# One block of A turned by DMA instead of TensorE, and the order of the first products that wait for it

## The chip, the cores and the metric

The kernel runs on one core of one Trainium2 chip. The metric is the device time of one execution in microseconds (us). A profile of one execution comes with the times. Its engines are called PE (TensorE), DVE (VectorE), ACT (ScalarE), POOL (GpSimd) and SP (the engine that only issues transfers here).

## The reference

```
x = a @ b                                  # 2048 x 2048 x 2048, float32 in
rms = sqrt(mean(x**2, axis=-1) + eps)      # one number for each row
out = gamma * x / rms                      # float32 out
```

## The kernel before, in words

**The product.** A is cut into 16 blocks of 128 rows, B into two halves of 1024 columns. TensorE needs A with the summed dimension on the partitions, so each block of A is turned (transposed) before it is used. Blocks 0 to 3 (the "head") are turned on TensorE while B still arrives. From block 4 on, two blocks make a group `g`, and each pair of a group and a half of B is computed by the Winograd form of Strassen's method: seven products of half size instead of eight, each 8 matmuls of 128x512, accumulated in banks of PSUM. `halves` numbers the pairs: n = 0 and 1 are the two halves of group 2 (blocks 4 and 5), n = 2 and 3 those of group 3 (blocks 6 and 7), and so on. `do(n, m)` issues product m of pair n. Products 1, 2 read quarters of the even block, so they need block 4 alone for n = 0 and 1; products 7, 6, 5, 3 read sums that `a_sums` makes on DVE from both blocks of the group, and product 4 a quarter of the odd block.

**Copies between products.** Several products go on accumulating on a copy of an earlier one. After product 1 ACT copies its bank to a second bank (`b2<-b1`, L591), after product 6 it copies that bank to a third (`b3<-b2`, L593), and products 5 and 3 go on in the third. `take(n, 11)` (L601) then copies the first bank to the result tile in SBUF. The banks are reused: pair n = 2 begins (product 1) in the bank that `take(0, 11)` has emptied into tile x_103, and x_103 must first have been stored to HBM with the previous rows that it held.

**How block 4 to 15 get turned.** A block is loaded as float32 (`load_block`, one transfer of 1 MB, issued by POOL), ACT takes the norms of its rows (`row_norm`), and DVE scales it to 16 bits. Blocks 4 and 5 are then turned on TensorE (`transpose_half`, L198, 8 transposes of 128x128 for each half) and copied from PSUM by `take_transposed` (L205). Blocks 6 and later go through `prepare` (L248 to L253): DVE scales each half (L252) and SP issues a transfer that turns it (`dma_start_transpose`, L253), two for each block.

**Rows finished.** `finish(mb)` multiplies a finished block by gamma and by its inverse norm on DVE (L314) and stores each half from SP (L317, 512 KB).

**What sets the order.** The schedule is by hand: each engine runs its instructions in the order of the program text. So a transfer of SP waits for all that stands before it on SP. On POOL, `wait_for` (L146) is a small copy that waits for a piece of data, and with it holds back the loads that stand behind it. Around the change the loads of blocks 6, 7 and 8 are issued one after the other (blocks 7 and 8 by the lines 550 and 620), and TensorE runs, after the last products of the head: block 4's transposes, four matmuls of `product_4`, do(0,1), block 5's transposes (`turn_next`), two more of `product_4`, do(0,2), do(0,7), do(0,6), do(1,1), do(0,5), do(0,4). Then `segment(1)` begins: do(1,6), do(0,3), do(1,2), do(2,1), do(1,7), do(1,5), do(1,4), and `segment(2)` with do(2,6).

Both kernels hold the same loop of the later groups; the short names below are used in what follows: T4 to T7 for the turning of blocks 4 to 7, load 6 to load 8 for the loads of these blocks.

Of the kernel before, what the change touches and what calls it, by code (L numbers as in the profile page):

```python
# [17 lines left out]
def kernel(  # L18
# [13 lines left out]
    nc = tc.nc  # L32
# [61 lines left out]
    def at(mb):  # L94
        return (at_even, at_odd)[(mb // 2) % 2][:, mb % 2]

    def copy_on(engine):
        return nc.scalar.copy if engine == "A" else nc.vector.tensor_copy

    def add(out, in0, in1, op=ALU.add):  # L100
        nc.vector.tensor_tensor(out=out, in0=in0, in1=in1, op=op)  # L101
# [30 lines left out]
    def load_block(mb):  # L132
        if mb == HB + 4:
            a32[mb] = head_flat[:, 2 * K:].bitcast(FP32)
        else:
            a32[mb] = a_pool.tile([P, K], FP32, name="a32")
        nc.gpsimd.dma_start(out=a32[mb], in_=a[mb * P:(mb + 1) * P, :])
# [7 lines left out]
    def wait_for(src):  # L145
        nc.gpsimd.tensor_copy(out=pace, in_=src)  # L146
# [47 lines left out]
    def transpose_half(mb, h, bank):  # L194
        view = bank.bitcast(FP16).rearrange("p (g m) -> p g m", m=P)
        for n in range(8):
            kt = h * 8 + n
            nc.tensor.matmul(  # L198
                view[:, n, :], a16[mb][:, kt * P:(kt + 1) * P], identity_h,
                is_transpose=True, start=(n == 0), stop=(n == 7),  # L200
            )
        return view

    def take_transposed(mb, h, view, copy):
        copy(out=at(mb)[:, h * 8:(h + 1) * 8, :], in_=view)  # L205
# [38 lines left out]
    def row_apply(mb):  # L244
        a16[mb] = a16_slot[mb]
        nc.vector.tensor_scalar_mul(out=a16[mb], in0=a32.pop(mb), scalar1=factor.pop(mb))
# [31 lines left out]
    def square_half(mb, h):  # L278
        square_of(mb, x_tile(mb, h))
# [4 lines left out]
    def take_pre(mb):  # L284

        pre_of[mb] = stat_pool.tile([P, 1], FP32, name="pre")
        add(pre_of[mb], msq[mb][:, 0:1], msq[mb][:, 1:2])
# [11 lines left out]
    def square_right(mb):  # L299

        square_half(mb, 1)
        rms_of[mb] = root(msq[mb][:, 2:3], pre_of.pop(mb))
# [6 lines left out]
    def finish(mb, order=(0, 1)):  # L309
        if mb not in inverse_of:  # L310
            inverse_of[mb] = inverse(rms_of.pop(mb))
        for h in order:
            x = x_half.pop((mb, h))
            nc.vector.scalar_tensor_tensor(  # L314
                out=x, in0=x, scalar=inverse_of[mb], in1=gamma_sb[:, h * HALF:(h + 1) * HALF],
                op0=ALU.mult, op1=ALU.mult)
            nc.sync.dma_start(out=rows(mb, h * HALF, (h + 1) * HALF), in_=x)  # L317
# [128 lines left out]
    def evict(groups, engines):  # L446
        for g, engine in zip(groups, engines):
            copy_on(engine)(out=x_chunk(*g), in_=banks[g])  # L448
# [85 lines left out]
    row_apply(HB)  # L534
    evict(plain[1:2], "D")
    row_factor(HB + 1)
    evict(plain[2:3], "A")
    product(PAIR, 1, 3, acc[0])
    product(PAIR, 1, 5, u4, start=False)

    def product_4(lo, hi):
        for kp in range(lo, hi):
            product_matmul(PAIR, 1, 4, u2, kp, False)
# [2 lines left out]
    turned = [transpose_half(HB, h, (tbank, acc[1])[h]) for h in range(2)]  # L546
    take_transposed(HB, 0, turned[0], nc.scalar.copy)
    take_transposed(HB, 1, turned[1], nc.vector.tensor_copy)
    row_apply(HB + 1)
    load_block(HB + 3)  # L550
    for r in range(HB):
        take_pre(r)
    evict(plain[3:], "A")
    square_right(0)
    product_4(2, 6)

    def turn_next():
        for h in range(2):
            view = transpose_half(HB + 1, h, (tbank, acc[2])[h])
            take_transposed(HB + 1, h, view, nc.vector.tensor_copy)  # L560

    def pair_ends():
        nc.scalar.copy(out=x21, in_=p7)
        nc.scalar.copy(out=x12, in_=u4)
        add(x22, x12, x21)
        add(x12, acc[0], x12)
        add(x21, u2, x21)

    halves = [(g, j) for g in range(G0, NG) for j in range(2)]
    B1, B2, B3, B7 = (acc[1], acc[0]), acc[3:5], (acc[6], acc[5]), acc[2]

    def chunks(n):
        g, j = halves[n]
# [2 lines left out]
    def do(n, m, copies=True):  # L578

        if n >= len(halves) or n < 0:  # L580
            return
        g, j = halves[n]
        b1, b2, b3 = B1[n % 2], B2[n % 2], B3[n % 2]
        if g >= G2:
            b1 = b2
        product(g, j, m, {1: b1, 2: b1, 3: b3, 4: b2, 5: b3, 6: b2, 7: B7}[m],
                start=m in (1, 7))
        if m == 1 and g >= G2:
            nc.scalar.copy(out=chunks(n)[0], in_=b2)
        elif m == 1:  # L590
            nc.scalar.copy(out=b2, in_=b1)  # L591
        elif m == 6:
            nc.scalar.copy(out=b3, in_=b2)  # L593
        elif m == 7 and copies:
            nc.scalar.copy(out=chunks(n)[2], in_=B7)  # L595

    def take(n, what, engine="A"):

        x11, x12, x21, x22 = chunks(n)
        if what == 11:  # L600
            copy_on(engine)(out=x11, in_=B1[n % 2])  # L601
        elif what == 12:
            copy_on(engine)(out=x12, in_=B3[n % 2])
        elif what == 22:
            add(x22, B3[n % 2], x21)
        else:
            add(x21, B2[n % 2], x21)
# [5 lines left out]
    def first_segment():  # L613
        n, g, j = 0, G0, 0
        nxt = 2 * g + 2
        do(n, 1)
        square_right(1)
        turn_next()
        product_4(6, KP)
        load_block(HB + 4)  # L620
        a_sums(g, (3, 1, 2), False)
        do(n, 2)
        do(n, 7, False)
        pair_ends()
        finish(0, (1,))
        row_norm(nxt)
        a_sums(g, (4,))
        prepare(nxt)
        finish(0, (0,))
        do(n, 6)  # L630
        do(n + 1, 1)
        do(n, 5)
        nc.scalar.copy(out=chunks(n)[2], in_=B7)
        take(n, 22)
        row_norm(nxt + 1)
        take(n, 11)
        finish(1)
        do(n, 4)
        take(n, 21)
        prepare(nxt + 1)  # L640
        square_half(2 * g + 1, j)

    X2, W2, Y2 = tbank, B1[1], B1[0]
# [5 lines left out]
    def segment(n):  # L649
        g, j = halves[n]  # L650
        ra, rb, nxt = 2 * g, 2 * g + 1, 2 * g + 2
        more = g + 1 < NG
        if g >= G2 and (g - G2) % 2 == 1 and j == 0:
            block_segment(n)
            return
        first = g >= G2 and (g - G2) % 2 == 0
        do(n, 6)
        own = nxt + (g == NG - 2)
        if j == 0:
            finish(ra - 1)  # L660
            row_norm(own)
        elif g == G0:
            square_right(r2)
        do(n - 1, 3)
        take(n - 1, 12)
        if j == 0:
            square_right(ra - 2)
            prepare(own)
            a_sums(g, (4,))
            finish(ra - 2, (0, 1) if g < NG - 2 else (0,))  # L670
        else:
            if not first:
                square_half(ra, 0)
            if g == G0:
                square_right(r3)
                finish(r2, (1, 0))
            elif g == G0 + 1:
                finish(r3, (1,))
            elif g == G2:
                b_two(4)  # L680
            elif not first and g > G2:
                finish(ra - 2)
        if g < G2:
            do(n, 2)
            take(n, 11)
        if g == G2 - 1 and j == 1:
            b_two(3)
            b_two(1)
        do(n + 1, 1)
        if j == 1 and g + 2 < NG:  # L690
            wait_for(at(nxt + 1)[:, KT - 1, 0:1])
            if G0 < g < NG - 3:
                load_block(nxt + 2)
                wait_for(a32[nxt + 2][:, 0:1])
            load_block(nxt + 3)
        if j == 1:
            if first:
                a_two_sums(g)
            a_sums(g + 1, (1, 2))
        do(n, 7)  # L700
        if j == 0 and g < NG - 2:
            row_norm(nxt + 1)
        if j == 1:
            a_sums(g + 1, (3,))
            if g == NG - 3:
                row_norm(nxt + 2)
        do(n, 5)
        take(n, 22)
        if j == 0 and g == NG - 2:
            finish(ra - 2, (1,))  # L710
        if j == 1:
            take_pre(rb)
            if not first:
                take_pre(ra)
        do(n, 4)
        take(n, 21)
        if j == 0:
            square_half(rb, 0)
            if g < NG - 2:
                prepare(nxt + 1)  # L720
            if g == G2:
                b_two(2)
        else:
            if g == NG - 3:
                prepare(nxt + 2)
            if not first:
                square_right(rb)
            if g == G0:
                finish(r3, (0,))
# [189 lines left out]
```

## Time and profile before

| | |
|---|---|
| median of 3 runs | 219.24 us (219.06 to 219.25) |
| the profiled execution | 219.5 us, of which the span is 217.7 |
| PE busy | 207.3 us, 95% of the span |
| DVE busy | 161.2 us, 74% |
| ACT busy | 112.9 us, 52% |
| POOL busy | 36.5 us, 17% |
| mean granted clock of PE | 0.992 |
| HBM read, written | 34.60 MB, 16.78 MB |

All times inside the profile count from the start of the span. A busy PE is one whose matmuls follow each other; the matmul records overlap, since one of 128x512 has a record of 379 ns and the next begins about 216 ns after it. The two lines of a group that tell most are its busy time and what ended the idle time before it.

### The profile page before, as it was taken

How to read it: one execution, taken by the hardware profiler on the slowest of the kernel's cores; microseconds unless marked ns; L12 is line 12 of the kernel's file. 1: busy time of each engine (PE TensorE's matmuls, PEld its weight loads, DVE VectorE, ACT ScalarE, POOL GpSimd, SP SyncE). 2: the span in 40 equal slices, each digit the busy share in tenths (PEclk: the TensorE clock that was granted, in tenths of full speed). 3: DMA queues.
4: the chain of work that ended last, by engine and by line, in shares of the span. 5: the costliest groups of instructions: out<-in, count | busy, mean ns of one | idle time of the engine just before them, and what ended most of it. 6: DMA issues, size and time to landing. Idle time of an engine off the chain costs nothing.

```text
span 217.7 us, 2953 instructions
## 1 busy us (share of the span) xinstructions
PE 207.3 (95%) x1000; PEld 96.9 (45%) x1020; DVE 161.2 (74%) x323; ACT 112.9 (52%) x222; POOL 36.5 (17%) x74
## 2 busy tenths in 40 slices
PE   7999999999999999999999999999999999999970
PEld 3545444444455444444444444444444444444420
DVE  1228669999887996989975899399859973385771
ACT  2110001810399566789635962585778551555771
POOL 7544333443001000200021001102020000000020
PEclk9999999999999999999999999999999999999996
DMA  7999999999948889889775985498995950040455
GB/s 149 168 200 207 199 205 205 209 208 212 397 201 266 327 218 308 243 350 246 228 220 173 359 252 96 193 225 263 293 301 157 288 217 0 0 193 3 193 189 196
DMA packets 37039, 46.60 MB, mean 214 GB/s; under 512 B 22560, under 2 KB 26656, under 8 KB 35744
## 3 DMA queue, kind: packets, MB, share of 16 engines
q0 software_dynamic: 10608, 23.86, 45.3%
q1 hardware_dynamic: 26144, 22.29, 34.5%
q10 hardware_dynamic: 272, 0.26, 0.3%
q8 instruction: 8, 0.13, 0.2%
q14 instruction: 7, 0.06, 0.1%
HBM read 34.60 MB, written 16.78 MB: 236 GB/s over the span
## 4 chain that ended last, share of the span: by engine, by line
PE 84%; DMA 9%; POOL 2%; issue 1%; ACT 1%; DVE 0%; ACTq 0%; POOLq 0%
PE acc L361 65%; PE acc L409 11%; DMA early<-in_a_dram 5%; DMA b<-in_b_dram 4%; PE acc L400 3%; PE tbank L400 2%; POOL b L115 1%; PE tbank L361 1%; PE tbank L438 1%; PE tbank L185 1%; POOL early L119 1%; ACT a L786 1%; PE acc L198 0%; PE tbank L198 0%; ACT sq L872 0%
## 5 line engine op out<-in xcount | busy, mean ns | idle before, releaser
L361 PEld LDWEIGHTS <-s 128*128 128x128 f16 (+1 forms) x312 | 30.5, 98 | 36.8
L275 ACT ACTIVATE sq<-x 128x1024 bf16<-128x1024 f32 (+1 forms) x33 | 33.2, 1006 | 19.6 <-DVE x L101 15.8
L409 PE MATMUL acc<-b,head_at 128*128 128x512 bf16 x171 | 42.1, 379 | 0.2
L314 DVE SCALAR_TENSOR_TENSOR x<-x,r,gamma_sb 128x1024 f32<-128x1024 f32 x28 | 35.0, 1281 | 0.5
L361 PE MATMUL acc<-b,head_at 128*128 128x512 bf16 x135 | 33.9, 379 | 0.3
L101 DVE TENSOR_TENSOR x<-acc,x 128x512 f32<-128x512 f32 x33 | 22.1, 686 | 11.4 <-PE acc L361 5.5
L361 PEld LDWEIGHTS <-head_at 128*128 128x128 f16 (+1 forms) x192 | 18.7, 98 | 22.2
L361 PE MATMUL acc<-b,at_even 128*128 128x512 bf16 x110 | 26.2, 379 | 0.1
L409 PEld LDWEIGHTS <-head_at 128*128 128x128 bf16 x176 | 16.9, 98 | 19.3 <-issue 0.3
L361 PE MATMUL acc<-early,s 128*128 128x512 bf16 x101 | 25.1, 379 | 0.1
L361 PEld LDWEIGHTS <-at_even 128*128 128x128 f16 x160 | 15.6, 98 | 19.0 <-ACT at_even L205 0.3
L361 PE MATMUL acc<-b,s 128*128 128x512 bf16 x99 | 23.8, 379 | 0.2
L227 ACT ACTIVATE sq<-a 128x1024 bf16<-128x1024 f32 x22 | 23.3, 1057 | 1.3 <-DMA a<-in_a_dram 0.9
L361 PE MATMUL acc<-t_left,s 128*128 128x512 bf16 x96 | 22.5, 379 | 0.1
L115 POOL DMA_DIRECT2D b<-in_b_dram x32 | 17.2, 540 | 20.0 <-DMA b<-in_b_dram 13.6
L448 ACT COPY x<-acc 128x512 f32<-128x512 f32 x7 | 4.0, 586 | 27.0 <-PE acc L409 27.0
L593 ACT COPY acc<-acc 128x512 f32<-128x512 f32 x12 | 6.9, 576 | 10.3 <-PE acc L361 10.3
L190 DVE COPY head_at<-tbank 128x1024 bf16<-128x1024 bf16 x7 | 4.8, 692 | 7.9 <-PE tbank L185 7.9
L296 DVE RECIPROCAL r<-rms 128x1 f32<-128x1 f32 x16 | 2.5, 159 | 10.6 <-ACT rms L291 10.6
L789 POOL TENSOR_SCALAR x<-x,r 128x512 f32<-128x512 f32 x2 | 1.4, 688 | 47.8 <-DVE r L296 47.8
L101 DVE TENSOR_TENSOR x<-tbank,x 128x512 f32<-128x512 f32 x9 | 6.2, 690 | 4.2 <-PE tbank L438 4.1
L595 ACT COPY x<-acc 128x512 f32<-128x512 f32 x10 | 5.8, 585 | 4.9 <-PE acc L361 3.8
(129 smaller groups left out, 243.7 us busy)
## 6 DMA issues: line engine op xcount, KB each, us to landing
out_dram<-x SPq DMA_DIRECT2D x29, 512.0 KB, 3.3
a<-in_a_dram POOLq DMA_DIRECT2D x9, 1024.0 KB, 5.6
b<-in_b_dram POOLq DMA_DIRECT2D x32, 256.0 KB, 10.0
a<-in_a_dram POOLq DMA_DIRECT2D x4, 512.0 KB, 9.8
early<-in_a_dram POOLq DMA_DIRECT2D x7, 256.0 KB, 10.0
gamma_sb<-in_gamma_dram POOLq DMA_DIRECT2D x2, 512.0 KB, 9.9
head_at<-in_a_dram POOLq DMA_DIRECT2D x1, 1024.0 KB, 7.1
out_dram<-x SPq DMA_DIRECT2D x3, 256.0 KB, 2.6
```

Source lines behind the costliest of these rows:

```text
L101: nc.vector.tensor_tensor(out=out, in0=in0, in1=in1, op=op)
L115: nc.gpsimd.dma_start(out=raw[j][kp][:, t, :], in_=b[lo:lo + P, j * HALF:(j + 1) * HALF])
L190: nc.vector.tensor_copy(out=head_at[:, 2 * kp:2 * kp + 2, :, :], in_=view)
L227: nc.scalar.activation(out=junk, in_=a32[mb][:, h * HALF:(h + 1) * HALF], func=ACTF.Square, scale=2.0 ** -8, accum_out=n2[:, h:h + 1])
L275: nc.scalar.activation(out=sq[:, 0:src.shape[-1]], in_=src, func=ACTF.Square, scale=inv_sqrt_n, accum_out=msq[mb][:, c:c + 1])
L314: nc.vector.scalar_tensor_tensor(out=x, in0=x, scalar=inverse_of[mb], in1=gamma_sb[:, h * HALF:(h + 1) * HALF], op0=ALU.mult, op1=ALU.mult)
L361: nc.tensor.matmul(bank, lhsT[:, kp, :], rhs, start=(start and kp == 0), stop=(kp == KP - 1), skip_group_check=not start)
L400: nc.tensor.matmul(bank, lhsT[:, k, :], rhs, start=(m in (1, 7) and k == 0), stop=(k == KQ - 1), skip_group_check=m not in (1, 7))
L409: nc.tensor.matmul(bank, head_at[:, kt, r, :], head_rhs(c, kt), start=(kt == 0), stop=(kt == KT - 1))
L448: copy_on(engine)(out=x_chunk(*g), in_=banks[g])
L593: nc.scalar.copy(out=b3, in_=b2)
L595: nc.scalar.copy(out=chunks(n)[2], in_=B7)
```

## The change

Block 5 is no longer turned on TensorE. DVE scales its two halves one by one and SP issues a transposing transfer for each (new L551 and L552), as for the blocks behind it. A `wait_for` on the turned block now stands on POOL ahead of load 7, and load 8 follows load 7 at once. On TensorE, `product_4` is no longer split around the transposes, and do(1,1) and do(1,2) move up, so that the order is do(0,1), do(1,1), do(0,2), do(1,2), do(0,7), do(0,6), do(0,5), do(0,4). do(1,1) goes to the bank `tbank` that the transposes used. ACT's eviction of one bank of the head goes to DVE, the adds of `pair_ends` and the store of block 0's right half move ahead of `a_sums`, the fourth sum and one half of `finish(1)` move back, and `take(1, 11)` moves behind do(2,1).

```diff
     evict(plain[1:2], "D")
     row_factor(HB + 1)
-    evict(plain[2:3], "A")
     product(PAIR, 1, 3, acc[0])
     product(PAIR, 1, 5, u4, start=False)
...
-    row_apply(HB + 1)
+    src, f = a32.pop(HB + 1), factor.pop(HB + 1)
+    for h in range(2):
+        half = slice(h * HALF, (h + 1) * HALF)
+        nc.vector.tensor_scalar_mul(out=a16_first[:, half], in0=src[:, half], scalar1=f)
+        nc.sync.dma_start_transpose(at(HB + 1)[:, h * KP:(h + 1) * KP, :], a16_first[:, half])
+    wait_for(at(HB + 1)[:, KT - 1, 0:1])
     load_block(HB + 3)
     for r in range(HB):
         take_pre(r)
+    product_4(2, KP)
+    load_block(HB + 4)
+    nc.scalar.copy(out=x21, in_=p7)
+    nc.scalar.copy(out=x12, in_=u4)
     evict(plain[3:], "A")
-    square_right(0)
-    product_4(2, 6)
-
-    def turn_next():
-        for h in range(2):
-            view = transpose_half(HB + 1, h, (tbank, acc[2])[h])
-            take_transposed(HB + 1, h, view, nc.vector.tensor_copy)
-
-    def pair_ends():
-        nc.scalar.copy(out=x21, in_=p7)
-        nc.scalar.copy(out=x12, in_=u4)
-        add(x22, x12, x21)
-        add(x12, acc[0], x12)
-        add(x21, u2, x21)
+    add(x22, x12, x21)
+    add(x12, acc[0], x12)
+    add(x21, u2, x21)
+    evict(plain[2:3], "D")
...
+    def b1_of(n):
+        return tbank if n == 1 else B1[n % 2]
...
         do(n, 1)
+        square_right(0)
+        do(n + 1, 1)
         square_right(1)
-        turn_next()
-        product_4(6, KP)
-        load_block(HB + 4)
+        do(n, 2)
+        do(n + 1, 2)
+        finish(0, (1,))
         a_sums(g, (3, 1, 2), False)
-        do(n, 2)
         do(n, 7, False)
-        pair_ends()
-        finish(0, (1,))
         row_norm(nxt)
-        a_sums(g, (4,))
         prepare(nxt)
         finish(0, (0,))
         do(n, 6)
-        do(n + 1, 1)
         do(n, 5)
         nc.scalar.copy(out=chunks(n)[2], in_=B7)
         take(n, 22)
+        a_sums(g, (4,))
         row_norm(nxt + 1)
         take(n, 11)
-        finish(1)
+        finish(1, (0,))
         do(n, 4)
         take(n, 21)
         prepare(nxt + 1)
+        finish(1, (1,))
         square_half(2 * g + 1, j)
...
-        if g < G2:
+        if g < G2 and n > 1:
             do(n, 2)
             take(n, 11)
...
         do(n + 1, 1)
+        if n == 1:
+            take(n, 11)
```

More of the change, by code (lines that the diff above doesn't have):

```diff
@@ L582, in do @@
         g, j = halves[n]
-        b1, b2, b3 = B1[n % 2], B2[n % 2], B3[n % 2]
+        b1, b2, b3 = b1_of(n), B2[n % 2], B3[n % 2]
         if g >= G2:
@@ L600, in take @@
         if what == 11:
-            copy_on(engine)(out=x11, in_=B1[n % 2])
+            copy_on(engine)(out=x11, in_=b1_of(n))
         elif what == 12:
```

## The prediction

> **What bounds the kernel now.** I read the chain that ended last first, then the same chain in order of time, then each engine's timeline around the change, then the transfers. The chain by engine and by line (shares of the span):
>
> ```profile
> PE 84%; DMA 9%; POOL 2%; issue 1%; ACT 1%; DVE 0%; ACTq 0%; POOLq 0%
> PE acc L361 65%; PE acc L409 11%; DMA early<-in_a_dram 5%; DMA b<-in_b_dram 4%; PE acc L400 3%; PE tbank L400 2%; POOL b L115 1%; PE tbank L361 1%; PE tbank L438 1%; PE tbank L185 1%; POOL early L119 1%; ACT a L786 1%; PE acc L198 0%; PE tbank L198 0%; ACT sq L872 0%
> ```
>
> TensorE is the bound, and in order of time (start, length) the chain has no wait around the change:
>
> ```profile
> 67.80 0.45 PE tbank L198 x8
> 68.25 0.45 PE acc L198 x8
> 68.74 10.96 PE acc L361 x50
> ```
>
> So whatever leaves TensorE's queue is gained, and any wait on it is lost. The two L198 rows are block 5's transposes. The rows that a new wait would come from are ACT's copies and the matmuls after which they stand:
>
> ```profile
> 74.34 0.57 ACT L593 COPY acc<-acc 128x512 f32<-128x512 f32 x1 [1.03 <-PE acc L361]
> 83.31 0.59 ACT L601 COPY x<-acc 128x512 f32<-128x512 f32 x1 [1.92 <-DVE s L237]
> 84.50 1.89 PE L361 MATMUL acc<-b,head_at 128*128 128x512 bf16 x8
> ```
>
> L593 is the copy after do(0,6), L601 is take(0,11), the last row is do(2,1), which needs L601's bank. L601's idle time is put down to a DVE step that was long done; what it waited for is the store of x_103, issued at 79.94 and landing 3.3 us later, at 83.27. Last, the loads of blocks 6, 7 and 8 on POOL:
>
> ```profile
> 64.36 0.53 POOL L137 DMA_DIRECT2D a<-in_a_dram  x1 [9.20 <-ACT norm L230]
> 67.97 0.53 POOL L137 DMA_DIRECT2D a<-in_a_dram  x1 [3.08 <-ACT rms L291]
> 69.42 0.53 POOL L137 DMA_DIRECT2D head_at<-in_a_dram  x1 [0.92 <-PE acc L361]
> ```
>
> They land 5.2, 5.5 and 7.1 us after issue, at 69.6, 73.5 and 76.5: before T6 is issued (77.16).
>
> **Removed from TensorE.** The two L198 rows: 0.45 + 0.45 = 0.90 us, all on the path. With them go two DVE copies (L205, 0.69 each), while DVE gets an eviction (0.69) from ACT; both have room there, so nothing.
>
> **New wait 1: a copy that loses its cover.** do(0,5) accumulates on the bank that L593 fills from do(0,6)'s result. Before, do(1,1) stood between do(0,6) and do(0,5): 1.73 us of matmuls (8 of 0.216) hid the copy. Now do(1,1) is ahead and do(0,5) follows do(0,6) directly. In the rows, do(0,6)'s eight slots end at 74.14, the copy runs from 74.34 to 74.91; so the next product waits 0.77, and some 0.1 for the hand-over (block 4's copies L205 ended at 65.73 and 65.86 and do(0,1) began at 65.91). Taken: 0.85 us; bounds 0.75 and 0.95. It eats the gain: -0.90 + 0.85 = -0.05.
>
> **New wait 2: is block 5 turned in time?** T5's first half is scaled when DVE has finished L205 (65.86): L252's 0.744 gives 66.53, the second half 0.77 later. SP issues T5a at 66.60; T6's two issues stand 1.45 apart (77.16, 78.61), so T5b at 68.05. T6b to T9b, undisturbed, land 4.5 to 4.85 after their block's first issue: 71.1 to 71.45. But load 6 is in flight until 69.56. The trace has two pairs issued into a load. At 144.02 the load landed at 146.93, the pair at 149.72, 2.8 later. The other:
>
> ```profile
> 151.85 1.24 SPq L253 DMA_TRANSPOSE at_even<-a_half  x1
> 153.26 3.18 SPq L253 DMA_TRANSPOSE at_even<-a  x1
> ```
>
> landed at 158.46, 1.8 after its load (156.65). The DMA queue table of the window 152.9 to 155.0 has one line (packets, MB, share of 16 engines), POOL's queue alone:
>
> ```profile
> q0 software_dynamic: 77, 0.63, 85.8%
> ```
>
> So a transfer that is issued behind a load is served after it. For T5b that gives 71.4 to 72.4; I take 71.8, with 71.1 to 72.4 as ends. On TensorE, 38 matmuls (six of `product_4`, four products) now stand from 64.97 on: 38 x 0.216 = 8.2, so do(0,7) is due at 73.17 and do(0,6) at 74.90. `a_sums` makes its three sums at 0.72 apart from 71.9: 72.6, 73.3, 74.0. In time by 0.5 and 0.9. Cost 0; each us by which T5b is later than 72.4 costs one.
>
> At this step stands a rule that speaks against the change. The row: 16 transposes in 0.90 us, 0.056 each. The Trainium skill, "VectorE: DVE Perf Modes", section "Rules for kernel authors", says to turn 128x128 on TensorE where PSUM will do as the destination and by DMA otherwise, and "The three transpose paths" gives 390 ns against 1309 ns. An estimate from that page would be 6.2 us off TensorE and 21 us until block 5 is there, some 14 us too late; the trace's pair needs 4.5 to 4.85, so I don't use it.
>
> **New wait 3: the loads move into T6.** Loads 7 and 8 now stand behind `wait_for` on T5b. T7 landed at 88.8 in the trace, its L146 began at 88.89 and the load behind it was issued at 89.53: 0.73 after landing. So load 7 goes out at 72.55 (4.6 later than before) and load 8 directly behind (0.53 of issue). Load 8 landed 8.55 after load 7's issue (67.97 to 76.5): now 81.1. Meanwhile T6 is ready at about its old time. On ACT, `row_norm(6)` now stands behind the copy after do(1,1) (69.9) and `square_right(1)`, so it begins near 71.9 and, with 2.66 as in the trace, ends at 74.6; DVE needs 0.7 from L235 to L252 and 0.74 for that: T6a at 76.1, T6b at 77.5. Both go behind load 8. By the two pairs above they land 1.8 to 2.8 after it: 82.9 to 83.9. Behind T6 on SP and in its queue is x_103's store. In the trace it landed 1.27 after T6b (82.0 to 83.27): now 84.2 to 85.2, mid 84.7, where 83.27 stood before. L601's copy and hand-over (0.04 + 0.58 + 0.1) let do(2,1) begin at 85.4. TensorE is due there at 84.50 - 0.90 + 0.85 = 84.45 (before, it had 0.6 to spare). Stall 0.95; with both T5 ends 71.1 to 72.4 and 1.8 to 2.8 it is 0 to 2.05.
>
> A rule weighs on this. The row: two stores issued at 119.58 and 120.78, into a load, land after 4.3 us where others take 2.6 to 3.3, and of 120.4 to 121.2 the queue table shows POOL's queue alone:
>
> ```profile
> q0 software_dynamic: 38, 0.31, 106.4%
> ```
>
> The skill's "DMA: Bandwidth & Descriptors", section "Rules for kernel authors", says that rings of two engines interleave by packet on the same 16 engines. By that, T6's packets of 256 bytes would pass one by one between load 8's of 8 KB, and nearly all of T6 would still come after it: the same sum, within 0.1. The trace shows no interleaving.
>
> **What follows.** ACT's chain after L601 (squares, L291, then DVE's L314 and `a_sums` of group 3, done at 90.92, 7.61 after L601's start) feeds do(2,6), which began at 91.41, 6.91 after do(2,1). With L601 at 84.75 the sums come at 92.36, and do(2,6) at 85.4 + 6.91 = 92.31 waits another 0.1. Later loads are paced by their own blocks and move along; T7 queues behind the two stores and lands near 89.3, ahead of its use at 91.5.
>
> **Sum.** -0.90 + 0.85 + 0 + 0.95 + 0.1 = +1.0. The profiled execution, 219.5 (span 217.7 and 1.8 around it), is 0.26 above the median; on the median 219.24 + 1.0 = 220.2.
>
> **Rivals.** *Not slower:* the DMA engines serve T6 and x_103's store ahead of load 8, or load 8 is quick. It decides at a landing of x_103's store by 83.75: then do(2,1) starts at 84.45, and the sum is -0.90 + 0.85 = -0.05, 219.2. For it: T5b at its early end with the short gap reaches 83.5. Against: no transfer in this trace passes a load. Chance 0.22. *T5 late:* a pair blocked on SP for 2.4 to 3.2 us, as in the two rows; T5b at 73.6 leaves the first sum at 74.4 against 73.17 (1.2 lost), and x_103's store at 86.5, do(2,1) at 87.2: +2.75 in all, 222.0. For it: load 6 is in flight; against: it ends soon after T5a. Chance 0.13. *Faster:* wait 1 is smaller than read and wait 3 absent. Even a free hand-over leaves L593's 0.57, so -0.3; more than the 0.44 (0.2%, about what a measurement of this kernel can tell from no change) needs a slack that I don't see. Chance 0.05. The forecast has 0.60.
>
> **The numbers.** Forecast, with T5b's and the gap's ends: 219.2 to 221.3. To reach 8 in 10 the range takes in the on-time case and most of the late one: 219.0 to 221.9. Faster by over 0.2%: 0.06. Within: 0.24 (on time 0.20 and the low end of the forecast 0.04). Slower: 0.70.
>
> **What would show it.** In the profile after: no L198 on block 5; a TensorE gap of 0.85 before do(0,5), ended by the copy after do(0,6); load 7 issued near 72.6; T6 landing after load 8, near 83.4; a gap near 1 before do(2,1), ended by ACT's copy into x_103. Wrong if do(0,5) follows without a gap, if T6 lands by 81.5, or if the copy into x_103 starts by 83.8. A granted clock below 1 between 70 and 95 would also break it: in the trace it falls once, to a mean of 0.53 in 214 to 217, after matmuls have been absent since 210.8, and no gap above is that long.

## The result, and the profile after

| | before | after |
|---|---|---|
| median of the runs compared | 219.23 us (219.06 to 220.34, 6 runs) | 221.89 us (221.11 to 222.49, 6 runs) |
| ratio after to before | | 1.0108, 95% interval 1.0083 to 1.0133 |
| the profiled execution | 219.5, span 217.7 | 221.11, span 219.3 |
| PE busy | 207.3 us | 207.9 us |
| mean granted clock of PE | 0.992 | 0.995 |

The change makes the kernel slower by 2.66 us on the medians. The profiled execution of after is the shortest of the six, so it shows less of the loss than the median has; a second profile, below, is of a longer one.

The waits of TensorE, in the profile after (what waited, for what: us in total, times, longest). None of the three rows exists before:

```profile
PE acc L361 <- ACT x L602: 1.2, 1, 1.2
PE acc L361 <- ACT acc L594: 0.7, 1, 0.7
PE acc L361 <- DVE s L338: 0.2, 1, 0.2
```

The chain that ended last, in order of time (start, length), in the stretch where before had one unbroken row of matmuls:

```profile
67.42 4.75 DMA at_even<-a_first
72.26 0.70 DVE s L338
73.01 3.64 PE acc L361 x16
76.67 0.58 ACT acc L594
77.30 3.63 PE acc L361 x16
81.08 3.75 DMA out_dram<-x
84.91 0.59 ACT x L602
85.55 53.83 PE acc L361 x248
```

The path now leaves TensorE three times: for T5 and the first sum of `a_sums` (before do(0,7)), for the copy after do(0,6) (before do(0,5)), and for the store of x_103 and the copy into it (before do(2,1)). Eight matmuls take 1.727 us from start to start, so the starts give the whole loss of each gap, the hand-over included: 0.35, 0.83 and 1.35 us, and 0.13 before do(2,6). With the 0.90 us that the transposes no longer take this is +1.76. From the start of block 4's transposes to the start of the last product the profile after takes 1.78 us more than the one before (146.53 and 144.75), so behind these gaps nothing more is lost. The two profiled executions differ by 1.61, since the one of after began block 4's transposes 0.51 earlier and ran 0.33 longer behind the start of its last product; what made these two differences was not looked into.

SP's queue and POOL's queue in the timeline of after (start, length, instruction):

```profile
66.04 4.01 SPq L552 DMA_TRANSPOSE at_even<-a_first  x2
75.84 1.36 SPq L253 DMA_TRANSPOSE head_at<-a_half  x1
77.31 3.72 SPq L253 DMA_TRANSPOSE head_at<-a  x1
81.08 1.24 SPq L317 DMA_DIRECT2D out_dram<-x  x2
```

```profile
73.20 0.53 POOL L137 DMA_DIRECT2D a<-in_a_dram  x1 [0.80 <-DVE s L338]
73.72 0.53 POOL L137 DMA_DIRECT2D head_at<-in_a_dram  x1
```

Loads 7 and 8 now go out at 73.2 and 73.7, the second lands at 81.3, and T6, issued into them, lands at 83.6. Behind T6 stands x_103's store. ACT's copy into x_103 shows the wait by its idle time in brackets:

```profile
84.91 0.59 ACT L602 COPY x<-acc 128x512 f32<-128x512 f32 x1 [3.99 <-DMA out_dram<-x]
```

The row to learn from is the third of SP's: an issue that took 1.24 to 1.34 us for T6 and T7 in the profile before occupied SP for 3.72, and the store stood behind it. The same issue in the profile before:

```profile
78.61 1.27 SPq L253 DMA_TRANSPOSE head_at<-a  x1
```

The first of SP's rows of after hides the same: two issues in 4.01 us, of which the first took 1.32 and the second 2.63. The DMA queue tables of after (packets, MB, share of 16 engines), first of 69 to 70 and then of 70 to 71, have one line each and show what that did to T5:

```profile
q1 hardware_dynamic: 35, 0.01, 29.7%
```

```profile
q1 hardware_dynamic: 845, 0.21, 95.1%
```

From 69 to 70 almost nothing was moved at all, by any queue. By 70, 520 of T5's 2,112 packets had gone, a quarter; the rest began to flow just behind the end of SP's issue, at 70.05, and T5's second half landed 2.12 us after that end.

### The profile page after: what moved, and what is told of

It reads as the page before. It is cut to its first block, busy times and chain, and to the rows that moved or that the text cites. A ratio compares the mean times of both kernels' runs of the same rounds, so it can differ in the third digit from the quotient of the medians.

```text
span 219.3 us, 2943 instructions
## 1 busy us (share of the span) xinstructions
PE 207.9 (95%) x1004; PEld 95.6 (44%) x1004; DVE 160.9 (73%) x323; ACT 112.4 (51%) x221; POOL 36.8 (17%) x75
## 4 chain that ended last, share of the span: by engine, by line
PE 86%; DMA 7%; ACT 2%; issue 1%; DVE 1%; POOL 1%; SPq 0%; ACTq 0%; DVEq 0%; POOLq 0%
PE acc L361 60%; PE acc L409 16%; DMA early<-in_a_dram 3%; PE acc L400 3%; PE tbank L400 2%; DMA at_even<-a_first 2%; PE tbank L438 2%; DMA out_dram<-x 2%; PE tbank L185 2%; PE tbank L361 1%; ACT a L788 1%; POOL b L115 0%; DVE head_at L190 0%; DVE s L338 0%; ACT x L602 0%
## 5 line engine op out<-in xcount | busy, mean ns | idle before, releaser
L409 PE MATMUL acc<-b,head_at 128*128 128x512 bf16 x176 | 43.0, 379 | 0.1
L361 PE MATMUL acc<-b,head_at 128*128 128x512 bf16 x136 | 33.9, 379 | 1.2 <-ACT x L602 1.2
L361 PE MATMUL acc<-early,s 128*128 128x512 bf16 x104 | 25.6, 379 | 0.0
L361 PE MATMUL acc<-b,s 128*128 128x512 bf16 x104 | 24.4, 379 | 0.0
L361 PE MATMUL acc<-b,at_even 128*128 128x512 bf16 x96 | 22.7, 379 | 0.7 <-ACT acc L594 0.7
L448 ACT COPY x<-acc 128x512 f32<-128x512 f32 x6 | 3.4, 592 | 26.1 <-PE acc L409 26.1
L296 DVE RECIPROCAL r<-rms 128x1 f32<-128x1 f32 x16 | 2.6, 161 | 11.6 <-ACT rms L291 11.6
L146 POOL CAST pace<-at_even 128x1 f32<-128x1 f16 x4 | 1.8, 444 | 45.5 <-DMA at_even<-a 37.7
```

Source lines behind the costliest of these rows:

```text
L361: nc.tensor.matmul(bank, lhsT[:, kp, :], rhs, start=(start and kp == 0), stop=(kp == KP - 1), skip_group_check=not start)
L409: nc.tensor.matmul(bank, head_at[:, kt, r, :], head_rhs(c, kt), start=(kt == 0), stop=(kt == KT - 1))
```

## The experiments

The theory at the start: the TensorE time is really saved; the copy without cover costs 0.83; T5 and the two loads that it holds back push T6 and x_103's store late. Rivals: the new order costs by itself, or the transfers can be rearranged so that nothing waits. Where nothing else is said, a diff is against the changed kernel.

**The copy gets its cover back.** The median of before beside these first four experiments was 219.10 us.

```diff
         do(n, 6)
+        do(n + 1, 6)
         do(n, 5)
...
-        do(n, 6)
+        if n > 1:
+            do(n, 6)
```

> The changed kernel with do(1,6) moved between do(0,6) and do(0,5), so that 1.73 us of matmuls lie over the copy L594. Theory (the waits are in series and the store of x_103 sets the end of the stage): the gap of 0.83 before do(0,5) goes, do(2,1) is due 0.8 earlier, finds x_103 stored at the same time as before, and its gap grows from 1.35 to about 2.2. Time as the changed kernel within 0.3: 221.6 to 222.2. Rival (each gap has its own price): 0.83 less, 221.1, with the gap before do(2,1) still at 1.35.

Measured: 222.84 us, ratio 1.016 (1.0132 to 1.0189); the profiled execution 221.41. The gap before do(0,5) is gone, and do(2,1) starts 0.38 us later than in the profile of after, with a longer idle time:

```profile
85.93 1.89 PE L361 MATMUL acc<-b,head_at 128*128 128x512 bf16 x8 [2.46 <-ACT x L602]
```

So the two waits stand in series: what is gained at the first is waited out at the second, where the gap is now 2.62 us from start to start. The time is 0.6 above the range that was expected. The other executions are longer still, 222.3 to 223.9; the four longest have a mean clock of 0.981 to 0.983, against 0.988 in the profiled one (see the third experiment).

**Load 8 held back until T6 has landed.**

```diff
     product_4(2, KP)
-    load_block(HB + 4)
...
         prepare(nxt)
+        load_after(at(nxt)[:, KT - 1, 0:1], HB + 4)
```

> The changed kernel with load 8 held back on POOL until block 6 is turned (load_after on T6). Theory (T6 and x_103's store wait behind load 8 in the transfers): T6 lands near 80.5 instead of 83.6, L602 starts near 82.4 instead of 84.9, the gap before do(2,1) goes; left are -0.90 for the transposes, +0.35 before do(0,7) and +0.83 before do(0,5): +0.3 against the kernel before, 219.5, that is 1.5 to 2.4 below the changed kernel. Rival (T6 is slow by itself: SP needs 3.7 us to issue its second half, whatever else is in flight): L602 no earlier than 84.5, time as the changed kernel.

Measured: 221.93 us, ratio 1.0126 (1.011 to 1.0142). Half of the expectation holds: x_103's copy starts at 83.23, and do(2,1) follows without a gap. But the 219.5 is missed, and the time is that of after: load 8, issued at 82.56, now lies in front of T7, and the wait has moved to the sums of group 3 and do(2,6):

```profile
91.53 0.69 DVE L338 TENSOR_TENSOR head_at<-head_at 128x1024 f16<-128x1024 f16 x1 [2.07 <-DMA head_at<-a]
93.06 1.90 PE L361 MATMUL acc<-t_left,s 128*128 128x512 bf16 x8 [1.38 <-DVE s L338]
```

**Both edits together,** the diffs of the first and the second experiment.

> Both edits: do(1,6) over the copy, and load 8 held until block 6 is turned. Theory: only the transposes' 0.90 and the 0.35 before do(0,7) are left, -0.55: 218.7, faster than the kernel before. do(2,1) is due near 83.4 on the profile's clock and L602 ends near 83.0, so up to 0.3 may be left of its gap. Rival (gaps with their own price and T6 slow by itself): 221.1.

Measured: 223.24 us, ratio 1.0153 (1.0114 to 1.0191), in two groups: 220.93 and 221.13, and four of 223.2 to 223.5. The profile is of the second group; a row of TensorE and one slice of the windows view (length, then busy share of PE, PEld, DVE, ACT, POOL, granted clock, DMA share, GB/s):

```profile
93.07 2.78 PE L361 MATMUL acc<-t_left,s 128*128 128x512 bf16 x8 [2.03 <-DVE s L338]
```

```profile
94.00:95.00 1.00, 1.00 (x4) 0.38 (x3) 1.00 (x4) 0.00 (x0) 0.00 (x0) 0.50 1.31 328
```

After a gap of 2.2 us (start to start) the granted clock was 0.50 for 3.4 us, and the 16 matmuls that fell into it took 1.7 us longer. Between the two groups lie some 2.3 us; the drop explains 1.7 of them, and as no execution of the shorter group was profiled, the rest stays open. In that group the two edits bring 0.8 to 1.0 us against after's median; they do not reach before.

**The new order alone, first attempt.** The order of after on the kernel before, with block 5 still turned on TensorE; the diff is against the kernel before.

```diff
         do(n, 2)
-        do(n, 7, False)
         pair_ends()
+        do(n + 1, 1)
+        do(n + 1, 2)
+        do(n, 7, False)
...
         do(n, 6)
-        do(n + 1, 1)
         do(n, 5)
```

> The kernel before (block 5 turned on TensorE, loads 7 and 8 where they were) with only the products moved: do(1,1) and do(1,2) ahead of do(0,7), do(1,1) in tbank, do(0,5) directly behind do(0,6). Theory: the one thing added is the uncovered copy after do(0,6): +0.83, 220.05, with a gap of 0.8 before do(0,5) and none before do(2,1). Rival (the new order of products by itself upsets the later groups): over 220.6, with gaps elsewhere.

Measured: 222.15 us, ratio 1.0142 (1.0121 to 1.0163). This does not give the price of the order: my edit had left DVE's adds of `pair_ends`, which read banks of the head, behind three sums. They end at 73.22, ACT's copy of do(1,1)'s result into such a bank begins at 73.31, after 3.08 us of idle time, and do(1,2) waited 1.88 us for it.

**The new order alone, second attempt.** The transposes stand in other banks. Part of this kernel's output is not the reference's, and why was not settled, so it is read for its times alone. The diff shows the main lines, against the changed kernel. Before: 219.53 us.

```diff
...
+    def turn_next():
+        for h in range(2):
+            view = transpose_half(HB + 1, h, (acc[6], acc[2])[h])
+            take_transposed(HB + 1, h, view, nc.vector.tensor_copy)
...
         square_right(0)
+        turn_next()
         do(n + 1, 1)
```

> The new order of products and copies with block 5 still turned on TensorE (in banks that are free by then, so that no copy of ACT stands late), loads 7 and 8 as in the kernel before. Theory: one uncovered copy, +0.83: 219.9 to 220.3, a gap of 0.8 before do(0,5), none above 0.2 elsewhere. Rival (the order itself upsets the groups behind): over 220.6.

Measured: 220.26 us, ratio 1.0032 (1.0017 to 1.0047), +0.73. The copy after do(0,6) is the one new wait of any size.

**The new order alone, whole.** The transposes in `tbank` and acc[2], each copied out before its bank is used again. The diff is against the second attempt. Before: 219.24 us.

```diff
-            view = transpose_half(HB + 1, h, (acc[6], acc[2])[h])
+            view = transpose_half(HB + 1, h, (tbank, acc[2])[h])
...
         do(n + 1, 1)
-        square_right(1)
         do(n, 2)
+        square_right(1)
```

> The new order of products (1 and 2 of both halves first) on the kernel before, with block 5 still turned on TensorE; the transposes of the second half stand in a bank of their own, which ScalarE copies out before do(1,1) begins. Theory (the copy that loses its cover costs its own length, the order itself nothing): do(0,5) begins 0.8 us late behind the copy of do(0,6)'s accumulator, up to 0.4 us more are lost before do(1,1), where the bank must be empty, and no other gap appears: 220.0 to 220.6. Rival (the order upsets the later groups): gaps behind do(0,5) in do(2,1) or do(2,6), over 220.8.

Measured: 220.57 us, ratio 1.0057 (1.0039 to 1.0076). The waits of TensorE behind the head:

```profile
PE acc L361 <- ACT acc L594: 0.7, 1, 0.7
PE tbank L361 <- DVE at_even L205: 0.4, 1, 0.4
```

From start to start they cost 0.83 and 0.57 us, 1.40 together, against 1.33 measured. do(2,1) and do(2,6) follow without a gap. The 0.57 belongs to the transposes, which the changed kernel does not have; the order costs the copy that it uncovers, and nothing later.

**The transfers alone.** T5 by DMA, with TensorE's order of before.

```diff
-        do(n + 1, 1)
         square_right(1)
         do(n, 2)
-        do(n + 1, 2)
...
         do(n, 6)
+        do(n + 1, 1)
         do(n, 5)
```

> Block 5 turned by DMA as in the changed kernel, but TensorE's order as before: do(0,1), do(0,2), do(0,7), do(0,6), do(1,1), do(0,5). Theory: do(0,7) is due at 69.2 on the profile's clock and its sum comes at 72.9 to 73.4, a gap of 3.6 to 4.2 in one place, none before do(0,5), and the one before do(2,1) gone, as TensorE is later than the store: 222.0 to 223.5, more where the clock drops after so long a gap. Rival (the loss comes from the order of products): near 219.5.

Measured, beside 219.53 of before: 223.39 us, ratio 1.019 (1.0151 to 1.023). The profile is of the shortest of the four executions, 222.55; the two longest have a mean clock of 0.981 and 0.982, against 0.988 in the profiled one.

```profile
68.58 1.89 PE L361 MATMUL acc<-b,at_even 128*128 128x512 bf16 x8 [0.70 <-ACT acc L592]
73.28 3.63 PE L361 MATMUL acc<-t_left,s 128*128 128x512 bf16 x15 [2.81 <-DVE s L338]
```

Without do(1,1) and do(1,2) ahead of do(0,7), TensorE waits 2.97 us (start to start) for T5's sums. The moved products are therefore worth having as soon as block 5 comes by DMA. The copy before do(0,2) (0.86 us), which the transposes used to hide, I had not expected.

**Load 8 later still,** behind T7, with the first experiment's cover. Before: 219.53 us.

```diff
     product_4(2, KP)
-    load_block(HB + 4)
...
             wait_for(at(nxt + 1)[:, KT - 1, 0:1])
+            if g == G0:
+                load_block(HB + 4)
```

> The changed kernel with do(1,6) over the copy and load 8 held until block 7 is turned, so that neither T6 nor T7 nor x_103's store stands behind it. Theory: only do(0,7)'s gap of 0.35 to 0.65 is left beside the 0.90 saved: 218.6 to 218.9, faster than the kernel before. Rival (the transfers are full until about 100, so a load that is put off comes late for its own block): block 8's norms or its turning are late, and the wait turns up before do(4,1): 219.5 to 221.

Measured: 224.44 us, ratio 1.0209 (1.0174 to 1.0244). The rival had the kind of loss right, not its size: it named 221 at most. The waits are now spread from do(0,7) to 140 us: ACT, for one, sat 3.11 us until block 8 had landed. So 91.17 is no better place for load 8 than 82.56 was. That there is no room at all is not shown: from 80 to 85 the DMA share of this run is 0.56, and a place between the two was not tried.

**Loads 7 and 8 not held back by T5.** Before, for this and the next: 219.24 us.

```diff
-    wait_for(at(HB + 1)[:, KT - 1, 0:1])
     load_block(HB + 3)
```

> The changed kernel without the wait for block 5's transfers on GpSimd's queue: loads 7 and 8 are issued as early as in the kernel before. Theory (transfers are served in order of arrival and fill the queue): the second half of block 5's transfers comes behind load 7, or behind both loads, and lands at 76 to 79 instead of 72 to 73; do(0,7) waits 3 to 6 us for it, and the store bound by x_103 is on time again: 222.5 or more. Rival (the transfers of block 5, issued first, are served first, and the wait on GpSimd was what cost): they land at 72, no gap before do(0,7), none before do(2,1), about 219.5.

Measured: 228.93 us, ratio 1.0447 (1.0408 to 1.0485).

```profile
80.17 6.08 PE L361 MATMUL acc<-t_left,s 128*128 128x512 bf16 x16 [7.05 <-DVE s L338]
```

```profile
66.33 4.68 SPq L552 DMA_TRANSPOSE at_even<-a_first  x2
```

The issue of T5's second half began at 67.72, that of load 7 only at 67.88, and still T5 landed last, at 79.3, 11.6 us after the start of its issue. It was not quite ahead, though: that issue occupied SP for 3.30 us, until 71.02, and both loads were issued meanwhile. do(0,7) lost 7.2 us and then ran at a granted clock of 0.50 (6.08 us for 16 matmuls instead of 3.62). With -0.90 and 0.83 that makes 9.6; the profiled execution, 229.24, is 10.0 above before's median. So the wait on POOL, which costs the later stores their time, buys much more than it costs. The queue table of 74 to 76:

```profile
q0 software_dynamic: 100, 0.69, 82.5%
q1 hardware_dynamic: 100, 0.03, 5.6%
```

As many packets of one queue as of the other, the loads' mostly of 8 KB and the transposing transfer's of 256 bytes, so T5 got 0.03 of 0.72 MB. That is the rule of the Trainium skill, "DMA: Bandwidth & Descriptors", section "Rules for kernel authors" (rings of two engines interleave by packet), and in these 2 us the trace agrees with it.

**Block 5 not turned.** No transfers for it and no wait on POOL, with the first experiment's cover.

```diff
-        nc.vector.tensor_scalar_mul(out=a16_first[:, half], in0=src[:, half], scalar1=f)
-        nc.sync.dma_start_transpose(at(HB + 1)[:, h * KP:(h + 1) * KP, :], a16_first[:, half])
-    wait_for(at(HB + 1)[:, KT - 1, 0:1])
+        dst = at(HB + 1)[:, h * KP:(h + 1) * KP, :].rearrange("p t m -> p (t m)")
+        nc.vector.tensor_scalar_mul(out=dst, in0=src[:, half], scalar1=f)
```

> The changed kernel with do(1,6) between do(0,6) and do(0,5) as cover for the copy, and with block 5 not turned at all: VectorE's scaled block stands where the turned one would, with no transfers and no wait on GpSimd, so the rows that rest on block 5 are not the reference's. Theory (only the transfers and the uncovered copy cost): no gap on TensorE from 64 to 95 us, and the 0.9 us of the sixteen transposes are gained in full: 218.2 to 218.5. Rival (the order of products costs by itself, or the gain of TensorE is lost later to another bound): 219.2 or more.

Measured: 218.84 us, ratio 0.9991 (0.9977 to 1.0006): between the theory and its rival. All the waits of after are gone, and one is new. First DVE's row and TensorE's in this kernel, then DVE's row in the kernel before:

```profile
89.97 0.69 DVE L338 TENSOR_TENSOR s<-head_at 128x1024 f16<-128x1024 f16 x1
90.72 1.90 PE L361 MATMUL acc<-t_left,s 128*128 128x512 bf16 x7 [0.52 <-DVE s L338]
```

```profile
90.23 0.69 DVE L338 TENSOR_TENSOR s<-head_at 128x1024 f16<-128x1024 f16 x1
```

The second sum of group 3, which do(2,6) needs, ends 27.0 us after block 4's transposes begin; in before it was 26.9. TensorE came earlier by 0.90, DVE did not, and before do(2,6) had only 0.49 to spare. Of the 0.90, then, at most about 0.4 could be had in this order even if block 5 were turned for nothing. (+0.69 lost at do(2,6) against -0.90 is -0.21; the medians differ by -0.40; the interval of the ratio includes 1.)

**Half of load 6.** Before: 219.53 us.

```diff
+        width = HALF if mb == HB + 2 else K
-        nc.gpsimd.dma_start(out=a32[mb], in_=a[mb * P:(mb + 1) * P, :])
+        nc.gpsimd.dma_start(out=a32[mb][:, 0:width], in_=a[mb * P:(mb + 1) * P, 0:width])
```

> The changed kernel with load 6 cut to half its size: only the left half of block 6 is loaded, and stands for the right half too, so the rows of block 6 are not the reference's; everything else is the same work. Theory (the wait for block 5 comes from load 6, behind which its transfers land): load 6 lands near 67, block 5's transfers at 71.0 to 71.6 in place of 72.2 to 73.1, do(0,7) begins without a gap, load 7 goes out near 72 and the store bound by x_103 lands about 1.2 us earlier; the gap before do(2,1) falls to 0 to 0.6, the one of 0.8 before do(0,5) stays: 219.2 to 220.2. Rival (the transfers need their 72 to 73 by themselves, whatever is in flight): they land as before, with the same gaps, 221.2 to 222.5.

Measured: 221.27 us, ratio 1.0074 (1.0052 to 1.0095). The time and the gap before do(2,1) are the rival's: T5 landed at 72.0, and do(2,1) still lost 1.94 us. Only do(0,7) begins as the theory had it, with a gap of 0.05. SP's rows (this kernel's lines are numbered 4 higher):

```profile
66.15 3.83 SPq L556 DMA_TRANSPOSE at_even<-a_first  x2
...
77.19 4.26 SPq L257 DMA_TRANSPOSE head_at<-a  x1
```

Even the load of 512 KB took 4.9 us, to 68.9, and T5's second issue 2.33 us, to 69.98. So the amount of the load moves T5 little. T5 landed 2.0 us after the end of its own issue, as in after, and that issue ended 1.1 us after the load had landed, so the load's landing is not what frees SP.

**After, profiled a second time.** This execution took 222.81 us.

> The changed kernel once more, for a second profile beside the first: the first profiled execution is the shortest of six (221.11, where the median is 221.89), and its gaps sum to less than the median's loss. Theory (the transfers set the end of the stage, and they vary): the gap before do(2,1) is the one that differs, 1.3 to 2.6 us, the copy's gap stays at 0.83 and do(0,7)'s at 0.3 to 0.7. Rival (the rest is somewhere behind this stage): the same gaps as in the first profile and a longer way from do(2,6) to the end.

```profile
PE acc L361 <- ACT x L602: 1.8, 1, 1.8
PE acc L361 <- DVE s L338: 1.0, 1, 1.0
PE acc L361 <- ACT acc L594: 0.7, 1, 0.7
```

```profile
66.19 4.92 SPq L552 DMA_TRANSPOSE at_even<-a_first  x2
```

The same three waits, with two of them longer. T5's issues took 0.91 us more and T5 landed at 73.1; from start to start do(0,7) lost 1.17 us and do(2,1) 2.0, do(0,5) again 0.83. With 0.13 before do(2,6) and -0.90 that is +3.2, against 3.28 over before's median of 219.53. The two profiled executions of after enclose the median.

## Why the prediction was right, and where it was short

It forecast 220.2 and slower; the median is 221.89, at the upper end of the range. The direction, the wait for the uncovered copy and the chain of the third wait were forecast with their causes. That the median still lies inside the range is luck: it does so by 0.01 us, and the loss is 2.66 us where +1.0 was forecast. What came out is nearer to the rival "T5 late", to which I gave 0.13, than to the forecast, to which I gave 0.60. Step by step:

- *Transposes removed, -0.90:* right; no other engine's time comes back for it. That DVE's chain before do(2,6) would have taken half of it was in the rows (sums at 90.92, do(2,6) at 91.41), but I did not draw that conclusion. It did not matter here, since the waits are larger.
- *Wait 1, 0.85:* measured 0.83, in both profiles of after.
- *Wait 2, 0:* this is the step that failed. I took T5 to land 5.2 us after its first issue (71.8 less 66.60; the ends 71.1 and 72.4 are 4.5 and 5.8). It took 6.1 and 6.95 us, outside both ends, and do(0,7) lost 0.35 and 1.17. I had reasoned that load 6 would end soon, and placed T5 behind its landing. What the profiles show is an issue that occupies SP for 2.63 and 3.53 us for the second half, after which it still needs 2.0 to 2.1 to land. The row for this was on my page (153.26, 3.18 us), and I used it only for the rival "T5 late". That rival named a loss of 1.2 at do(0,7) and 222.0 in all; the second profile has 1.17, and the median is 221.89. I had also held load 6 to its 5.2 us of before. With T5 beside it, it took 6.7 and 7.5.
- *The rule behind wait 2* (T5 lands 1.8 to 2.8 us after load 6 has landed): in both profiles of after it came 1.6 us after, but with half of load 6 it came 3.1 us after, so that landing is not what T5 waits for. One of the two pairs that gave the rule was misread as well: the second issue of the pair at 144.02 began only at 146.62, when its load had 0.3 us left, and landed 3.1 us later, as one with no load in flight (3.1 to 3.4 for T6 and T7 of before). The 2.8 us are no wait behind a load; the long step there is the pair's first issue, 2.44 us.
- *Wait 3, 0.95:* the chain was the right one, link by link, and the absolute times in the profiled execution fit: T6 landed at 83.6 (forecast 82.9 to 83.9) and the copy into x_103 began at 84.91 (84.75). But that profile runs 0.5 us early, as block 4's transposes show (63.56 instead of 64.07), so TensorE was due earlier, and the gap was 1.35; in the other, 2.0. The excess is T5's lateness handed on: load 7 goes out 1.0 after T5's landing, and all behind it moves along. Nor did T6 or the store pass load 8, so the rival "not slower" fell, though what I held against it was not so: in the trace before, a store issued at 89.57 landed at 93.93, ahead of the load that was issued 0.04 us before it and landed at 96.70.
- *do(2,6), 0.1:* measured 0.13.

The sum was therefore short by one term, T5's landing, which enters twice: at do(0,7) and again through loads 7 and 8 at do(2,1). Replacing it by the measured gaps gives +1.76 and +3.2 for the two executions, and their mean, 2.5, is close to the 2.66 of the medians.

My sentence that the trace shows no interleaving of packets was too broad: the experiment without the wait shows it one for one. In 78 to 80 of after, on the other hand, with T6 issued at 75.84 and 77.31, the table has 94 packets of the load against one:

```profile
q0 software_dynamic: 94, 0.77, 104.0%
q1 hardware_dynamic: 1, 0.00, 0.1%
```

Why T6's packets were not there yet, so long after the issue, stays open. That SP's blocked issue is what makes T5 late rests on times: in the two profiles of after, in that of half of load 6 and in the five others with T5's transfers and the wait on POOL, T5 lands 2.0 to 2.1 us after SP is free, and meanwhile the DMA engines are nearly idle (the table of 69 to 70 above; in the second profile 19 packets from 70 to 71), so T5 was not waiting for a load's packets then. Without the wait on POOL, with two loads beside it, it landed 8.3 us after. Why the second issue is held so long was not measured by itself, so the cause behind it stays open. Issuing T5 from another queue wasn't tried.

## What to carry to other kernels

When a step moves from an engine to the DMA queues, look first for what else those queues do at that moment, then follow each issue on the queue that makes it, since a blocked issue also delays every store behind it. A transfer that is late pays once for each reader, and again for each load that was told to wait for it. Before counting an engine's saved time as gained, subtract the chain of the other engines into the next meeting point: here DVE's chain left at most about 0.4 of the 0.9 us.

## What the runs showed of the hardware

- An issue of a transposing transfer (128x1024, 16 bits) occupied SP for 1.24 to 1.34 us in T6 and T7 of before, with no load by POOL in flight. T5's second half, issued while load 6 was in flight, took 2.33 to 3.53 in nine profiles, and 2.33 is the one with a load of 512 KB; T6's second half took 3.72 to 4.36 with loads 7 and 8 in flight (after, twice; the cover; the transfers alone; half of load 6), and 1.27 to 1.80 with load 7 alone in flight (the three runs with load 8 held back). A load in flight does not settle it: first issues of a pair took up to 2.44 too (144.02 of before), and one at 125.92 of after took 2.46 when no load had been in flight for 1.1 us.
- A transposing transfer whose issue began 0.2 us ahead of a load of 1 MB, and lasted 3.3 us, was overtaken by it and by the next: 11.6 us from the start of the issue to landing.
- A gap on TensorE of 2.2 us was followed by a granted clock of 0.50 for 3.4 us in the profile of the two edits together, which cost 1.7 us; the mean clocks of its executions (0.981 to 0.987 in the four long ones, 0.990 and 0.994 in the two short ones) suggest the same for the other three long ones, which were not profiled. Gaps of 2.0 (after, the second profile), 2.62 (the cover) and 2.97 us (the transfers alone) passed without a drop in the executions profiled. The Trainium skill, "TensorE: Matmul & The Clock Gate", section "🎯 Why this matters for your kernels", warns of gaps above some 3 us; here one of 2.2 was enough. My prediction had relied on no gap being long enough.
